# First MLP product of a Conformer layer by seven block products, with the residual stream kept in DRAM meanwhile

## The chip, the core and the metric

The kernel runs on one core of a Trainium2 chip. A core has five engines that work side by side, each on its own list of instructions in the order in which the list was written: PE (matrix products; its weight loads are shown apart as PEld), DVE (vector work), ACT (activations and copies), POOL (slower vector work) and SP (which here only issues transfers). They meet through semaphores. The metric is the device time of one execution in microseconds (us), the median of three runs; one further execution was profiled.

## The reference

One layer on 512 tokens of width 2048, all in float32, then a last RMSNorm:

```python
h = rmsnorm(x, norm1_g)
x = x + conformer_conv(h, ...)                  # w_in, GLU, 31-tap conv, layernorm, silu, w_out
x = x + square(relu(rmsnorm(x, norm2_g) @ w1)) @ w2   # w1 2048 x 8192, w2 8192 x 2048
return rmsnorm(x, final_g)
```

The change concerns the product with `w1` and what stands right before and behind it.

## The kernel before, in words

**Number format.** Every matrix product is split for accuracy: each operand becomes a high part (a cast to float32r) and a low part (the operand less its high part), and `mm3` (L282) adds three matmuls in one PSUM bank: high x high, high x low, low x high. Each of the three loads its own 128x128 stationary block.

**Stages.** The w_in projection and the convolution come first, then the w_out projection, whose first column group is done in a hand-written order with `ps`, and whose other three groups (q = 1 to 3, from L750) leave the residual stream `xt` with features on partitions (16 tiles of 128 features x 512 tokens). Then the first MLP product: `h2` holds the 16 tiles, scaled by the norm's gain and split into high and low (L768); for each of 64 blocks of 128 hidden features (`f`, L796) 16 x 3 matmuls of 128x512 sum over the 16 k-tiles into one bank. After the first block come the row scales of the norm (`row2`) and 64 transposes that turn `xt` into the residual with tokens on partitions, 16 tiles `x2` that stay in SBUF as `acc`.

**Hidden activations.** DVE applies relu and the row scale (L829), ACT squares (L830). Two blocks make a pair (32 pairs, 256 hidden features each). For 30 of the pairs, POOL forms four sums of the pair's blocks of 256 tokens (`s1` to `s4`, L840 to L843), ACT casts the seven factors to their high parts, DVE makes the low parts, and both are written to DRAM (`spill`). The second product needs them in that form.

**Second MLP product.** It already works by seven block products (`seven`, L856): a product of 2x2 blocks is formed with seven block products in place of eight, at the cost of sums on both sides. The factors of w2 are made while it runs: `Factor.make` (L153) forms differences on POOL (`less`, L158, 128x1024 in place), casts on ACT (L177), and for the low part either subtracts on POOL (`LO_POOL`, L179) or lets ACT copy the high part to PSUM twice (L183, bank `ax`) and DVE subtract in halves (L184). The activations' factors come back from `spill` by `fetch` (L789), issued on POOL into seven slots; three slots (pairs 0 to 2) are filled during the first product (at f = 8, 10, 12), pairs 3 to 6 from its end on.

**What sets the order.** `Stream` (L186) makes weight tiles four items ahead of their use; there are four buffers each for the high and the low parts (`wh`, `wl`), so the buffer of an item is the one that was used four items before. `LOAD` issues loads three items further ahead on SP. Outside the hand-written part (`manual_schedule`) a list scheduler orders each engine's instructions by the program order and by its own estimates; the engines then keep to that order.

Of the kernel before, what the change touches and what calls it, by code (L numbers as in the profile page):

```python
# [18 lines left out]
P = 128  # L19
# [49 lines left out]
LO_POOL = ("P2",)  # L69
# [13 lines left out]
def trunk(ctx: ExitStack, tc: tile.TileContext, xT, vec, fg, w_in, w_out, w1, w2s, w2b, out):  # L83
# [7 lines left out]
    big = ctx.enter_context(tc.tile_pool(name="big", bufs=16))  # L91
# [7 lines left out]
    early = right.enter_context(tc.tile_pool(name="early", bufs=1, side="right"))  # L99
    dram = ctx.enter_context(tc.tile_pool(name="dram", bufs=1, space=bass.MemoryType.DRAM))  # L100
# [26 lines left out]
    class Sums:  # L127


        def __init__(self, src):  # L130
            self.src = src
            self.raw = {}

        def buffer(self, b):

            pool, tag, n = (wts, "raw", 4) if b in ("22", "5") else (mlp[0], "rb", 8)
            return pool.tile([P, 1024], F32, tag=tag, name=f"b{b}", bufs=n)

        def get(self, b, hs):
            if (b, hs) not in self.raw:  # L140
                self.raw[b, hs] = t = self.buffer(b)
                nc.sync.dma_start(out=t, in_=self.src[BLOCKS.index(b), hs])
            return self.raw[b, hs]

    class Factor:
        def __init__(self, sums, product, hs):
            self.sums, self.product, self.hs = sums, product, hs
# [5 lines left out]
        def make(self, hi, lo):  # L153
# [24 lines left out]
            if self.product in LO_POOL:  # L178
                nc.gpsimd.tensor_tensor(out=lo, in0=s, in1=hi.bitcast(F32), op=sub)  # L179
                return  # L180
# [32 lines left out]
    for f in range(FF // P):  # L213
        items += [Plain(w1[f, c], nc.gpsimd if c else nc.vector) for c in range(2)]
    for g in range(NG):
        for q in range(2):
            sums = Sums(w2s[g, q])
# [3 lines left out]
    mlp = [None]  # L221
# [16 lines left out]
    mean1 = early.tile([P, P], F32, name="mean1")  # L238
# [4 lines left out]
    us = [early.tile([P, KC - 1 + T], F32, name=f"u{i}") for i in range(NU)]  # L243
# [46 lines left out]
    acc2 = early.tile([P, T], F32, name="acc2")  # L290
# [36 lines left out]

    def conv(j, pool_taps):

        u = us[j % NU]  # L330
        dj = big.tile([P, T], F32, tag="da", name=f"d{j}")
# [5 lines left out]
        for k in range(pool_taps):  # L337
            a, w = tap(k)
            prod = early.tile([P, T], F32, tag="prod", name="prod", bufs=3)
# [6 lines left out]
            if pacc is None:  # L346
                pacc = early.tile([P, T], F32, tag="pacc", name="pacc", bufs=2)
# [42 lines left out]
    with tc.manual_schedule():  # L390
# [45 lines left out]
        row1 = early.tile([P, T], F32, tag="row", name="row1", bufs=2)  # L436
# [24 lines left out]
    diags = early.tile([P, max(*PE_TAPS, 1), P], F32, tag="dg", name="dg", bufs=1)  # L461
# [19 lines left out]
    dl = big.tile([P, T], F32, tag="da", name="dl")  # L481
    held = None

    class Half:
# [30 lines left out]
        def act_taps(self, lo, hi):  # L515
            for k in range(lo, hi):
                a, w = self.tap(k)
                prod = early.tile([P, H], F32, tag="prod", name="prod", bufs=3)
                nc.scalar.activation(out=prod, in_=a, func=AF.Copy, scale=w)
                if k == 0:  # L520
                    self.pacc = early.tile([P, H], F32, tag="pah", name="pah", bufs=2)
# [74 lines left out]
        def put(self, i, cols):  # L596
# [6 lines left out]
            if i == 0:  # L603
                self.mean = early.tile([P, H], F32, tag="row", name="mean", bufs=2)
                nc.scalar.copy(out=self.mean, in_=self.rows[:, :H])
# [143 lines left out]
    h2 = [None] * NT  # L749
    for q in range(4):  # L750
        if q:
            ps = [bank() for _ in range(4)]
            for c in range(8):
                w = chunk()
                for i in range(2):
                    k = 2 * c + i
                    out_mm(ps, [x[:, i * 512 : (i + 1) * 512] for x in w], k, slice(0, T), k == 0, k == NT - 1)
        for n in range(4):
            j = 4 * q + n
            nc.vector.scalar_tensor_tensor(out=xt[j], in0=ps[n], scalar=col(V_BOUT, j), in1=xt[j], op0=ALU.add, op1=ALU.add)  # L760
            if j == 0:
# [5 lines left out]
    for j in range(NT):  # L767
        h2[j] = split_scaled(xt[j], col(V_G2, j), "y")  # L768


    NPAIR = FF // P // 2
    LASTS = NPAIR - GROUP // 4
    spill = [dram.tile([P, 2, 7 * HT], F32, name=f"spill{n}") for n in range(NPAIR)]
    acc = []
    row2 = None
    pairs = {}
    later = []

    def split(n, x, sl):

        width = sl.stop - sl.start
        hi = mlp[0].tile([P, 4 * HT], F32R, tag="rb", name="ah", bufs=8)
        lo = mlp[0].tile([P, 4 * HT], F32R, tag="rb", name="al", bufs=8)
        nc.scalar.copy(out=hi[:, :width], in_=x)
        nc.scalar.dma_start(out=spill[n][:, 0, sl], in_=hi[:, :width].bitcast(F32))
        nc.vector.tensor_tensor(out=lo[:, :width], in0=x, in1=hi[:, :width].bitcast(F32), op=ALU.subtract)
        later.append((spill[n][:, 1, sl], lo[:, :width].bitcast(F32)))

    def fetch(n):  # L789
# [3 lines left out]
        for y in range(2):  # L793
            nc.gpsimd.dma_start(out=pairs[n][y], in_=spill[n][:, y, :])

    for f in range(FF // P):  # L796
        ps = bank()
        for c in range(2):
            wh, wl = chunk()
            for i in range(8):  # L800
                k = 8 * c + i
                sl = slice(i * P, (i + 1) * P)
                mm3(ps, (wh[:, sl], wl[:, sl]), h2[k], k == 0, k == NT - 1)
        if row2 is None:
# [4 lines left out]
            r2 = spread(inv_sqrt(ms, eps_rms, RMS_EPS, NTOK))  # L809
            row2 = shift  # L810
            nc.scalar.copy(out=row2, in_=r2)

            for b in range(NTOK):
                for n in range(4):
                    x2 = big.tile([P, 512], F32, tag="da", name=f"x2_{b}_{n}")
                    pt = bank("ax")
                    for i in range(4):
                        nc.tensor.transpose(out=pt[:, i * P : (i + 1) * P], in_=xt[4 * n + i][:, b * P : (b + 1) * P], identity=ident)  # L818
                    nc.scalar.copy(out=x2, in_=pt)
                    acc.append(x2)  # L820
            right.close()
            mlp[0] = ctx.enter_context(tc.tile_pool(name="mlp", bufs=4, side="right", reuse_waits="tile"))
            slots = [ctx.enter_context(tc.tile_pool(name="slots", bufs=1, side="right", reuse_waits="tile"))] * 2
            slots.append(right.enter_context(tc.tile_pool(name="slot", bufs=1, side="right", reuse_waits="tile")))
        n = f // 2
        if f % 2 == 0:
            four = mlp[0].tile([P, 4 * HT], F32, tag="rb", name="four", bufs=8)
        here = four[:, f % 2 * T :][:, :T]
        nc.vector.scalar_tensor_tensor(out=here, in0=ps, scalar=0.0, in1=row2, op0=ALU.max, op1=ALU.mult)  # L829
        nc.scalar.activation(out=here, in_=here, func=AF.Square)  # L830
        for x in later:
            nc.scalar.dma_start(out=x[0], in_=x[1])
        later = []
        if n >= LASTS:
            split(n, here, slice(f % 2 * T, f % 2 * T + T))
        elif f % 2:
            a21, a11, a22, a12 = (four[:, i * HT : (i + 1) * HT] for i in range(4))
            sums = mlp[0].tile([P, 4 * HT], F32, tag="rb", name="sums", bufs=8)
            s3, s1, s2, s4 = (sums[:, i * HT : (i + 1) * HT] for i in range(4))
            nc.gpsimd.tensor_tensor(out=s3, in0=a11, in1=a21, op=ALU.subtract)  # L840
            nc.gpsimd.tensor_tensor(out=s1, in0=a21, in1=a22, op=ALU.add)
            nc.gpsimd.tensor_tensor(out=s2, in0=s1, in1=a11, op=ALU.subtract)
            nc.gpsimd.tensor_tensor(out=s4, in0=a12, in1=s2, op=ALU.subtract)  # L843
            split(n, four[:, HT:], slice(0, 3 * HT))
            split(n, sums, slice(3 * HT, 7 * HT))
        if f in (8, 10, 12):
            fetch((f - 8) // 2)
    for x in later:
        nc.scalar.dma_start(out=x[0], in_=x[1])
    left.close()  # L850
    late = ExitStack()
    slots += [late.enter_context(tc.tile_pool(name="slots2", bufs=1, reuse_waits="tile"))] * (SLOTS - 3)
    fetch(3)


# [35 lines left out]
    for g in range(NG - 1):  # L891
        for q in range(2):
# [3 lines left out]
    right.close()  # L896
    lasts = [ctx.enter_context(tc.tile_pool(name="lasts", bufs=1, side="right", reuse_waits="tile")),
             ctx.enter_context(tc.tile_pool(name="lasts2", bufs=1, reuse_waits="tile"))]
# [3 lines left out]
    def last_pair(n):  # L902
        for f in range(2):
            both = [lasts[0].tile([P, T], F32R, name="ah", tag=f"ah{len(a)}"),
                    lasts[0].tile([P, T], F32R, name="al", tag=f"al{len(a)}") if len(a) < 3 else mlp[0].tile([P, T], F32R, tag="rb", name="al", bufs=8)]
# [4 lines left out]
    for q in range(2):  # L910
        seven(NG - 1, q, 1)
        last_pair(LASTS + q)
        for n in (2 * q, 2 * q + 1):
            for m in range(4):
                raw = wts.tile([P, 1024], F32, tag="raw", name="raw", bufs=4)
                nc.sync.dma_start(out=raw[:, :512], in_=w2b[n, m])
                wh = lasts[1].tile([P, 512], F32R, tag=f"wh{n}{m}", name="w2h")
                wl = lasts[1].tile([P, 512], F32R, tag=f"wl{n}{m}", name="w2l")
# [10 lines left out]
    for b in range(NTOK):  # L929
# [6 lines left out]
        for i, cs in enumerate(pieces):  # L936
# [9 lines left out]
            sq = mlp[0].tile([P, 1024], F32, tag="rb", name="sq", bufs=8)  # L946
# [61 lines left out]
```

## Time and profile before

| What | Value |
|---|---|
| median of 3 runs (lowest, highest) | 1926.92 us (1924.57, 1929.64) |
| profiled execution: own time | 1929.75 us |
| profiled execution: span, first to last instruction | 1928.0 us |
| first MLP product, first to last matmul | 583.4 to 1290.2 us |
| second MLP product begins | 1290.9 us |
| DMA, mean over the span | 163 GB/s |

How to read it: the span lies between the first and the last instruction, and the rest of the execution's own time lies around it. Busy times of the engines overlap each other. A matmul's duration covers its way through the array, and the next one starts before it ends, so that the distance between two starts, not the duration, says what a row of matmuls takes. A group's line gives the instruction's line in the kernel, engine, operation, what it writes and reads with shapes, the count, the summed busy time, the mean of one in ns, and the idle time of the engine right before them with what ended it.

### The profile page before, as it was taken

The page shows a single profiled execution, that of the slowest core. Times are in us where ns is not written, and L with a number is a line of the kernel's source. Part 1 is how long each engine was busy: PE and PEld are TensorE (multiplying, and loading weights), DVE is VectorE, ACT ScalarE, POOL GpSimd, SP SyncE. Part 2 cuts the span into 40 slices and gives each one's busy share as a digit, 9 for nine tenths or more (in the row PEclk, how much of TensorE's full clock was granted, in tenths as well). Part 3 has the DMA queues.
Part 4 walks back from the last instruction along what each step waited for, and adds up shares of the span by engine and source line. Part 5 has one row for each costly group of instructions (what it writes and reads, how often), then busy time and mean ns, then how long its engine had stood idle before and what let it go on. Part 6 is the DMA issues. An engine that isn't in the chain of part 4 may idle for free.

```text
span 1928.0 us, 23365 instructions
## 1 busy us (share of the span) xinstructions
PE 1885.7 (98%) x8578; PEld 1565.3 (81%) x8578; DVE 1073.4 (56%) x1512; ACT 934.8 (48%) x1286; POOL 1122.3 (58%) x693
## 2 busy tenths in 40 slices
PE   6999999989999999999999999999999999999998
PEld 4888888988888888888888888887888888788776
DVE  8899999982034333332333333336665666556685
ACT  6444444464245333333333333346776677667762
POOL 5799999846553433434343333457567666686643
PEclk9999999989999999999999999999999999999999
DMA  5222233105222754554445544466746557457332
GB/s 217 84 99 88 99 120 113 63 13 206 98 95 101 272 199 174 183 195 181 178 172 187 193 175 175 181 215 232 250 143 240 193 189 274 132 217 245 127 103 98
DMA packets 87955, 314.33 MB, mean 163 GB/s; under 512 B 9760, under 2 KB 10400, under 8 KB 87840
## 3 DMA queue, kind: packets, MB, share of 16 engines
q1 hardware_dynamic: 59184, 197.41, 29.4%
q0 software_dynamic: 9792, 57.15, 8.4%
q10 hardware_dynamic: 18864, 58.27, 7.5%
q8 instruction: 67, 1.10, 0.2%
q14 instruction: 48, 0.39, 0.1%
HBM read 251.45 MB, written 61.34 MB: 162 GB/s over the span
## 4 chain that ended last, share of the span: by engine, by line
PE 84%; DVE 8%; POOL 4%; issue 3%; ACT 1%; DMA 1%; DVEq 0%; SPq 0%; POOLq 0%; ACTq 0%
PE mm L286 25%; PE mm L287 25%; PE mm L285 25%; PE mm L656 8%; POOL b L158 2%; DVE ax L361 1%; POOL wl L179 1%; DVE wl L184 1%; DVE x L874 1%; DVE xl L279 1%; DVE dl L545 1%; PE ax L818 0%; DMA b<-in_w2s 0%; DVE d L623 0%; DVE wl L125 0%
## 5 line engine op out<-in xcount | busy, mean ns | idle before, releaser
L125 POOL TENSOR_TENSOR wl<-raw,wh 128x1024 fp32r<-128x1024 f32 x151 | 365.5, 2431 | 464.1 <-ACT wh L124 447.6
L124 ACT CAST wh<-raw 128x1024 fp32r<-128x1024 f32 (+1 forms) x221 | 230.3, 1049 | 471.3 <-PE mm L286 369.2
L286 PE MATMUL mm<-yl,wh 128*128 128x512 f32 x1024 | 398.7, 389 | 0.2 <-DVE yl L279 0.2
L285 PE MATMUL mm<-yh,wh 128*128 128x512 f32 x1024 | 398.7, 389 | 0.0
L287 PE MATMUL mm<-yh,wl 128*128 128x512 f32 x1024 | 398.6, 389 | 0.0
L158 POOL TENSOR_TENSOR b<-b,b 128x1024 f32<-128x1024 f32 x120 | 288.7, 2417 | 148.7 <-DVE wl L184 83.5
L286 PE MATMUL mm<-wl,ah 128*128 128x512 f32 x840 | 327.7, 390 | 8.9 <-POOL wl L179 8.9
L285 PE MATMUL mm<-wh,ah 128*128 128x512 f32 x840 | 327.2, 390 | 1.2 <-DVE x L874 1.2
L287 PE MATMUL mm<-wh,al 128*128 128x512 f32 x840 | 326.7, 389 | 0.0
L184 DVE TENSOR_TENSOR wl<-b,ax 128x512 fp32r<-128x512 f32 x360 | 232.3, 684 | 129.4 <-ACT ax L183 115.1
L177 ACT CAST wh<-b 128x1024 fp32r<-128x1024 f32 x210 | 219.8, 1053 | 166.5 <-PE mm L287 149.2
L286 PEld LDWEIGHTS mm<-yl,wh 128*128 128x128 f32 x1024 | 192.2, 188 | 40.3 <-DVE yl L279 0.6
L285 PEld LDWEIGHTS mm<-yh,wh 128*128 128x128 f32 x1024 | 192.2, 188 | 39.8
L287 PEld LDWEIGHTS mm<-yh,wl 128*128 128x128 f32 x1024 | 192.2, 188 | 39.7
L361 DVE SCALAR_TENSOR_TENSOR ax<-u,v,ax 128x512 f32<-128x512 f32 x327 | 218.2, 753 | 0.0
L285 PE MATMUL mm<-xh,wh 128*128 128x512 f32 (+1 forms) x544 | 207.6, 382 | 5.1 <-ACT wh L124 5.1
L287 PE MATMUL mm<-xh,wl 128*128 128x512 f32 (+1 forms) x544 | 207.3, 381 | 4.0 <-DVE wl L125 4.0
L286 PE MATMUL mm<-xl,wh 128*128 128x512 f32 (+1 forms) x544 | 207.9, 382 | 1.6 <-DVE xl L279 1.6
L183 ACT COPY ax<-wh 128x512 f32<-128x512 f32 x360 | 200.3, 585 | 10.8 <-DVE wl L184 7.7
L874 DVE TENSOR_TENSOR x<-x,mm 128x512 f32<-128x512 f32 x224 | 149.6, 684 | 83.9 <-PE mm L287 83.9
L286 PEld LDWEIGHTS mm<-wl,ah 128*128 128x128 f32 x840 | 157.7, 188 | 44.5 <-POOL wl L179 12.2
L125 DVE TENSOR_TENSOR wl<-raw,wh 128x1024 fp32r<-128x1024 f32 (+1 forms) x70 | 87.9, 1256 | 184.1 <-ACT wh L124 184.1
(173 smaller groups left out, 2402.4 us busy)
## 6 DMA issues: line engine op xcount, KB each, us to landing
raw<-in_w SPq DMA_DIRECT2D x128, 512.0 KB, 3.2
b<-in_w2s SPq DMA_DIRECT2D x120, 512.0 KB, 4.5
raw<-in_w_in SPq DMA_DIRECT2D x63, 512.0 KB, 3.2
ah<-spill POOLq DMA_DIRECT2D x30, 896.0 KB, 5.7
al<-spill POOLq DMA_DIRECT2D x30, 896.0 KB, 8.0
raw<-in_w_out SPq DMA_DIRECT2D x32, 512.0 KB, 3.3
spill<-ah ACTq DMA_DIRECT2D x30, 512.0 KB, 2.6
spill<-al ACTq DMA_DIRECT2D x30, 512.0 KB, 2.7
```

The lines of the kernel that those rows point to most:

```text
L124: nc.scalar.copy(out=hi[:, sl], in_=raw[:, sl])
L125: (nc.vector if sl.stop == cut else self.eng).tensor_tensor(out=lo[:, sl], in0=raw[:, sl], in1=hi[:, sl].bitcast(F32), op=ALU.subtract)
L158: nc.gpsimd.tensor_tensor(out=raw[to, hs], in0=raw[x, hs], in1=raw[y, hs], op=sub)
L177: nc.scalar.copy(out=hi, in_=s)
L183: nc.scalar.copy(out=st, in_=hi[:, sl].bitcast(F32))
L184: nc.vector.tensor_tensor(out=lo[:, sl], in0=s[:, sl], in1=st, op=sub)
L285: nc.tensor.matmul(out=ps, lhsT=wh, rhs=xh, start=first, stop=False, **how)
L286: nc.tensor.matmul(out=ps, lhsT=wh, rhs=xl, start=False, stop=False, **how)
L287: nc.tensor.matmul(out=ps, lhsT=wl, rhs=xh, start=False, stop=last, **how)
L361: nc.vector.scalar_tensor_tensor(out=o, in0=a, scalar=w, in1=c, op0=ALU.mult, op1=ALU.add)
L656: nc.tensor.matmul(out=ps[n][:, sl], lhsT=a[:, wsl], rhs=x[:, sl], start=first and a is wh and x is hi, stop=last and x is lo)
L874: nc.vector.tensor_tensor(out=x2, in0=x2, in1=banks[x][s], op=ALU.add)
```

## The change

The first MLP product is done by seven block products too. The 16 k-tiles are taken as 8 pairs; `factors(p)` (new) scales a pair's two tiles on ACT, forms four sums of 128x256 on POOL, and then, for each of seven factors of 256 tokens, a high part on ACT and a low part on DVE. The weights come as `w1s`, four blocks of 128x1024 for each of 32 pairs of hidden blocks, and are made into seven factors by the same `Factor` code as w2 (products P2 and P3 take their low parts on POOL). A product of a pair is 8 x 3 matmuls of 128x256; seven of them, in three banks X, Y and Z, make a pair's four result blocks. DVE reads a bank after each product (L857 to L869 of the changed kernel), some reads twice over because a further sum is wanted.

The residual is transposed during the w_out projection (`residual`, 16 transposes for each column group) and is written to DRAM from ACT's queue; it is read back by 16 transfers on SP's queue after the first MLP product. All fetches of pairs 0 to 6 stand behind the first product. Buffers are laid out anew for this (`fore`, `prep`, `stage`, `res`).

```diff
+FIRST = (("P1", "P5", "P2", "P6", "P3", "P7", "P4"), ("P1", "P5", "P6", "P2", "P7", "P3", "P4"))
-LO_POOL = ("P2",)
+LO_POOL = (("P2", "P3"), ("P2",))
...
-    for f in range(FF // P):
-        items += [Plain(w1[f, c], nc.gpsimd if c else nc.vector) for c in range(2)]
+    for n in range(NPAIR):
+        sums = Sums(w1s[n], LO_POOL[0])
+        items += [Factor(sums, x) for x in FIRST[n > 0]]
...
+    def factors(p):
+        x = prep.tile([P, 4 * HT], F32, tag="x", name="xs", bufs=2)
+        for i in range(2):
+            nc.scalar.activation(out=x[:, i * T : (i + 1) * T], in_=xt[2 * p + i], func=AF.Copy, scale=col(V_G2, 2 * p + i))
...
+        nc.gpsimd.tensor_tensor(out=s1, in0=a21, in1=a22, op=ALU.add)
...
+            nc.scalar.copy(out=t[:, :HT], in_=f)
+            nc.vector.tensor_tensor(out=t[:, HT:], in0=f, in1=t[:, :HT].bitcast(F32), op=ALU.subtract)
+    def residual(n):
+        for b in range(NTOK):
...
+            nc.scalar.copy(out=x2, in_=pt)
+            nc.scalar.dma_start(out=acc[b][n], in_=x2)
...
+                    if q == 3 and k % 2 and k < 12:
+                        factors(k // 2)
+                if c == 1:
+                    residual(q - 1)
...
-    for j in range(NT):
-        h2[j] = split_scaled(xt[j], col(V_G2, j), "y")
...
-    for f in range(FF // P):
-        ps = bank()
...
-                mm3(ps, (wh[:, sl], wl[:, sl]), h2[k], k == 0, k == NT - 1)
+    for n in range(NPAIR):
+        banks = {x: bank() for x in "XYZ"}
...
+                mm3(x, tuple(h[:, sl] for h in w), (t[:, :HT], t[:, HT:]), product in OPENS and p == 0, p == 7, skip_group_check=True)
...
+                part(product, range(8), w)
+                read(product)
...
+        for x in (odd, even):
+            nc.scalar.activation(out=x, in_=x, func=AF.Square)
...
+            nc.gpsimd.tensor_tensor(out=s1, in0=z["21"], in1=z["22"], op=ALU.add)
...
-        if f in (8, 10, 12):
-            fetch((f - 8) // 2)
...
-    fetch(3)
+    for p in range(4):
+        fetch(p)
+    x2 = {}
+    for n in range(4):
+        for b in range(NTOK):
+            x2[b, n] = res.tile([P, 512], F32, name=f"acc{b}{n}")
+            nc.sync.dma_start(out=x2[b, n], in_=acc[b][n])
```

How the instructions stand now is shown for POOL and ACT in the middle of the first MLP product. Line numbers are those of each kernel's own file. First POOL before, one pair of hidden blocks: `wl` are low parts of w1, `sums` the four sums of the pair `four`.

```order
L125 TENSOR_TENSOR wl_6537<-raw_6538,wh_6536 128x1024
L840 TENSOR_TENSOR sums_6634<-four_6566 128x256
L125 TENSOR_TENSOR wl_6603<-raw_6604,wh_6602 128x1024
L841 TENSOR_TENSOR sums_6634<-four_6566 128x256
L842 TENSOR_TENSOR sums_6634<-sums_6634,four_6566 128x256
L843 TENSOR_TENSOR sums_6634<-four_6566,sums_6634 128x256
```

POOL now, one pair: `b11`, `b21`, `b12`, `b5`, `b22` are blocks of w1 and differences of them, `z` the finished pair of hidden blocks.

```order
L162 TENSOR_TENSOR b11_6480<-b22_6548,b5_6624 128x1024
L183 TENSOR_TENSOR wl_6696<-b21_6585,wh_6695 128x1024
L162 TENSOR_TENSOR b21_6585<-b21_6585,b11_6480 128x1024
L907 TENSOR_TENSOR sums_6730<-z_6478,z_6479 128x256
L908 TENSOR_TENSOR sums_6730<-z_6478 128x256
L909 TENSOR_TENSOR sums_6730<-sums_6730,z_6478 128x256
L910 TENSOR_TENSOR sums_6730<-z_6479,sums_6730 128x256
L183 TENSOR_TENSOR wl_6786<-b22_6548,wh_6785 128x1024
L162 TENSOR_TENSOR b5_6890<-b12_6783,b11_6746 128x1024
L162 TENSOR_TENSOR b12_6783<-b22_6814,b12_6783 128x1024
```

Where a pair had two 128x1024 operations and four small ones, it now has six and four (the two at the end belong to the pair after; that pair's own `b11` comes next), and the low part from `wh_6785` stands behind the sums.

ACT before, one pair: casts of w1 (`wh`), squares of `four`, casts and transfers of the pair's factors (`ah`, `spill`).

```order
L124 CAST wh_6572<-raw_6574 128x1024
L124 CAST wh_6602<-raw_6604 128x1024
L830 ACTIVATE four_6566<-four_6566 128x512
L784 CAST ah_6639<-four_6566 128x768
L785 DMA spill9_5030<-ah_6639 128x768
L784 CAST ah_6644<-sums_6634 128x1024
L832 DMA spill9_5030<-al_6640 128x768
L785 DMA spill9_5030<-ah_6644 128x1024
L124 CAST wh_6650<-raw_6652 128x1024
```

ACT now, at the same place: `ax` are the copies of high parts into PSUM.

```order
L181 CAST wh_6659<-b11_6480 128x1024
L181 CAST wh_6695<-b21_6585 128x1024
L187 COPY ax_6663<-wh_6659 128x512
L187 COPY ax_6666<-wh_6659 128x512
L900 ACTIVATE z_6479<-z_6479 128x512
L900 ACTIVATE z_6478<-z_6478 128x512
L914 CAST ah_6728<-z_6479 128x512
L914 CAST ah_6728<-z_6478 128x256
```

And right behind that:

```order
L181 CAST wh_6748<-b12_6517 128x1024
L914 CAST ah_6728<-sums_6730 128x1024
L187 COPY ax_6752<-wh_6748 128x512
L187 COPY ax_6755<-wh_6748 128x512
L181 CAST wh_6785<-b22_6548 128x1024
L181 CAST wh_6816<-b21_6585 128x1024
```

The cast of the sums (`ah_6728<-sums_6730`) now has copies of one weight factor and the cast of the next behind it in ACT's list, and the cast `wh_6695` stands right behind the cast of `b11_6480`, a block that POOL has just formed.

More of the change, by code (lines that the diff above doesn't have):

```diff
@@ L242, in trunk @@
     NU = 3
-    us = [early.tile([P, KC - 1 + T], F32, name=f"u{i}") for i in range(NU)]
+    us = [fore.tile([P, KC - 1 + T], F32, name=f"u{i}") for i in range(NU)]
     for u in us:
@@ L603, in put @@
             if i == 0:
[L604 removed]
+                self.mean = fore.tile([P, H], F32, tag="row", name="mean", bufs=2)
                 nc.scalar.copy(out=self.mean, in_=self.rows[:, :H])
@@ L808, in trunk @@
             nc.vector.tensor_scalar(out=ms, in0=st[:, :NTOK], scalar1=1.0 / D, scalar2=None, op0=ALU.mult)
[L809 to L830, printed above, removed]
+            nc.scalar.copy(out=row2, in_=spread(inv_sqrt(ms, eps_rms, RMS_EPS, NTOK)))
+        late = []
+        for product in FIRST[n > 0]:
+            w = chunk()
+            if n == 0 and product in LATE:
+                part(product, range(6), w)
+                late.append((product, w))
+                if product != LATE[-1]:
+                    continue
+                part("P1", (6, 7), late[0][1])
+                read("P1")
+                rows()
+                for x in late[1:]:
+                    part(x[0], (6, 7), x[1])
+                    read(x[0])
+            else:
+                part(product, range(8), w)
+                read(product)
         for x in later:
@@ L833, in trunk @@
         later = []
+        for x in (odd, even):
+            nc.scalar.activation(out=x, in_=x, func=AF.Square)
+        hi, lo = (stage.tile([P, 7 * HT], F32R, tag=x, name=x) for x in ("ah", "al"))
         if n >= LASTS:
[L835 to L838, printed above, removed]
+            parts = [(even, 0), (odd, 2)]
+        else:
+            sums = big.tile([P, 4 * HT], F32, tag="rb", name="sums")
```

162 lines of the change are left out of this document (104 added, 58 removed).

## The prediction

> **What bounds the kernel now.** I read the page's first part, then the busy time by stage, then the groups of instructions, each shape apart, and last the timeline. The page's first line names the engine:
>
> ```profile
> PE 1885.7 (98%) x8578; PEld 1565.3 (81%) x8578; DVE 1073.4 (56%) x1512; ACT 934.8 (48%) x1286; POOL 1122.3 (58%) x693
> ```
>
> By stage (start:end, length, then busy us of PE, PEld, DVE, ACT, POOL, granted clock, DMA share, GB/s), first the two product stages, w1 and then w2:
>
> ```profile
> 583.40:1290.90 707.50, 707.34 (x3153) 584.70 (x3152) 229.21 (x206) 244.24 (x285) 285.35 (x200) 1.00 0.50 184
> 1350.00:1875.00 525.00, 518.82 (x2280) 426.74 (x2279) 342.39 (x536) 374.38 (x526) 343.67 (x189) 1.00 0.55 193
> ```
>
> In the stage that is changed PE never waits, and POOL and ACT are busy for 40% and 35% of it. In the w2 stage, which already works by seven products, they are busy for 65% and 71%, and PE waits a little. What a matmul costs is read from the distance of two starts (start, duration), for 512 and for 256 columns; the 256-column ones are those of the convolution's last tile:
>
> ```profile
> 347.02 0.39 PE L285 MATMUL mm<-xh,wh 128*128 128x512 f32 x1
> 347.24 0.39 PE L286 MATMUL mm<-xl,wh 128*128 128x512 f32 x1
> 347.47 0.39 PE L287 MATMUL mm<-xh,wl 128*128 128x512 f32 x1
> ...
> 366.13 0.28 PE L286 MATMUL mm<-xl,wh 128*128 128x256 f32 x1
> 366.25 0.28 PE L287 MATMUL mm<-xh,wl 128*128 128x256 f32 x1
> 366.37 0.28 PE L285 MATMUL mm<-xh,wh 128*128 128x256 f32 x1
> ```
>
> So 0.227 and 0.120 us. The stage's 3 x 1024 matmuls take 3072 x 0.227 = 697 us of its 707.5; the other 10 are the 64 transposes and the row scales.
>
> **Part 1, PE's work.** Now 32 pairs x 7 products x 8 x 3 = 5376 matmuls at 0.120 = 645 us, 20.16 per pair. One product in eight is saved (87 us), but two half-length matmuls take 0.240, 0.013 more than a long one, so 52 us remain. The Trainium skill's page "TensorE: Matmul & The Clock Gate", section "Back-to-back issue gap", gives N/2.4 + 2.5 ns for a warm isolated gap, 109 ns for 256 columns and 216 for 512; by it the 5376 would take 586 us. The rows above have 120 and 227, with a weight load for each matmul, so the trace decides against that figure.
>
> **Part 2, who must keep up.** A pair now needs seven weight factors in 20.16 us, made by three engines. The prices are in the second product and in the sums of before (busy us, mean ns, idle before):
>
> ```profile
> L158 POOL TENSOR_TENSOR b<-b,b 128x1024 f32<-128x1024 f32 x120 | 288.7, 2417 | 148.7 <-DVE wl L184 83.5 <-DMA b<-in_w2s 55.1 <-issue 5.8
> L179 POOL TENSOR_TENSOR wl<-b,wh 128x1024 fp32r<-128x1024 f32 x30 | 71.9, 2398 | 43.0 <-ACT wh L177 43.0
> L841 POOL TENSOR_TENSOR sums<-four 128x256 f32<-128x256 f32 x30 | 43.5, 1452 | 0.0
> L843 POOL TENSOR_TENSOR sums<-four,sums 128x256 f32<-128x256 f32 x30 | 22.1, 737 | 2.4
> L177 ACT CAST wh<-b 128x1024 fp32r<-128x1024 f32 x210 | 219.8, 1053 | 166.5 <-PE mm L287 149.2 <-PE mm L286 13.2 <-DVE x L874 3.2
> L183 ACT COPY ax<-wh 128x512 f32<-128x512 f32 x360 | 200.3, 585 | 10.8 <-DVE wl L184 7.7
> L784 ACT CAST ah<-sums 128x1024 fp32r<-128x1024 f32 x30 | 31.5, 1051 | 124.7 <-POOL sums L843 124.7
> ```
>
> POOL, per pair: 4 differences x 2.417 + 2 low parts (P2, P3) x 2.398 + 4 sums x 0.737 = 17.4 us; with one sum at 1.452, as when DVE worked beside it, 18.1. That is under 20.16, but POOL has to wait twice in each pair, and both waits follow from the order. First: the low part of P3 stands behind the sums in POOL's list, and its high part stands in ACT's list behind the cast of those sums and the two copies of P7. From the last sum to that low part POOL stands still for 1.051 + 2 x 0.585 + 1.053 = 3.3 us. Second: the low part of P2 follows the difference for P6 in POOL's list, and ACT casts P6's factor, which POOL has just formed, before P2's: 2 x 1.053 = 2.1 us. ACT waits for POOL's sums and POOL for ACT, and neither passes over what waits. ACT's idle 124.7 us ahead of the cast of the sums shows it held there already, 4.2 us for each of 30, then without harm. The hand-overs are in the timeline:
>
> ```profile
> 904.22 0.74 POOL L842 TENSOR_TENSOR sums<-sums,four 128x256 f32<-128x256 f32 x1
> 905.04 0.74 POOL L843 TENSOR_TENSOR sums<-four,sums 128x256 f32<-128x256 f32 x1
> 905.81 1.05 ACT L784 CAST ah<-sums 128x1024 fp32r<-128x1024 f32 x1 [4.16 <-POOL sums L843]
> 905.87 0.33 ACTq L832 DMA_DIRECT2D spill<-al  x1
> ```
>
> 0.08 us from POOL to its own dependent next, 0.03 from POOL to ACT; some 14 steps at about 0.05 are 0.7. The ring of POOL and ACT closes in 17.4 to 18.1 + 3.3 + 2.1 + 0.7 = 23.5 to 24.2 us. P6's difference also overwrites the block whose low part DVE makes for P1, a wait that before does not show in this stage: 0 to 0.6. I take 24.0, with 22.8 (no hand-overs) and 24.8 as ends. PE then stands still for 3.8 us per pair, at P7 above all, which waits for its low part: DVE makes that behind the low part of the sums. The stage takes 32 x 24.0 = 768.
>
> DVE and ACT beside that:
>
> ```profile
> L184 DVE TENSOR_TENSOR wl<-b,ax 128x512 fp32r<-128x512 f32 x360 | 232.3, 684 | 129.4 <-ACT ax L183 115.1 <-issue 10.4 <-POOL wl L179 2.7
> L786 DVE TENSOR_TENSOR al<-sums,ah 128x1024 fp32r<-128x1024 f32 x30 | 36.8, 1226 | 100.3 <-ACT ah L784 100.3
> L628 DVE TENSOR_TENSOR d<-d,ax 128x256 f32<-128x256 f32 x30 | 12.4, 414 | 0.7 <-PE ax L602 0.7
> L830 ACT ACTIVATE four<-four 128x512 f32<-128x512 f32 x64 | 40.1, 626 | 0.0
> ```
>
> DVE: 10 half low parts x 0.684, 10 short reads of banks x 0.414, low parts of 1792 columns at 1.226 for 1024: 13 us. ACT: 7 casts x 1.053, 10 copies x 0.585, 2 squares x 0.626, casts of 1792 columns at 1.051 for 1024, 2 issues x 0.33: 17 us. Both fit and cost nothing beyond the ring. SP's loads of w1 keep their number and size.
>
> **Part 3, the start of the stage.** Each `factors(p)` has 2 scalings, 7 casts and 7 low parts of 128x256; the nearest rows:
>
> ```profile
> L278 ACT ACTIVATE yh<-xr,v 128x512 fp32r<-128x512 f32 x16 | 11.3, 722 | 14.3 <-PE mm L656 14.3
> L631 ACT CAST vh<-vj 128x256 fp32r<-128x256 f32 x32 | 13.0, 407 | 1.0
> L818 PE MATMUL ax<-ident,xr 128*128 128x128 f32 x64 | 9.3, 285 | 0.0
> ```
>
> ACT: 2 x 0.722 + 7 x 0.407 = 4.3 us. The last two, behind the final column group, are 8.6, covered by the first three products over six of eight k-pairs, 3 x 18 x 0.120 = 6.5; with the sums behind them I take 6 us of waiting (0 to 12). Stage: 774, against 707.5, +66.
>
> **Part 4, the w_out stage** takes over 48 of the 64 transposes: 48/64 x 9.3 = 7 us on PE, which the 774 above no longer holds. ACT has 6 x 4.3 = 26 us of factors in the last group's 192 x 0.227 = 43.6, beside casts, 16 issues x 0.33 for the residual's transfers and the copies that empty the transposes' two banks: a little waiting. +8 (5 to 14).
>
> **Part 5, the start of the second product.** Before, pairs 0 to 2 lay ready and 3 to 6 were fetched at its start:
>
> ```profile
> 1290.90:1322.00 31.10, 31.10 (x139) 25.75 (x138) 20.75 (x32) 23.90 (x34) 14.37 (x13) 1.00 0.96 349
> ```
>
> Waits in the second product (total, times, longest), and one of the page's DMA rows:
>
> ```profile
> POOL b L158 <- DMA b<-in_w2s: 52.4, 8, 12.0
> ...
> PE mm L286 <- POOL wl L179: 8.9, 7, 2.5
> ```
>
> ```profile
> ah<-spill POOLq DMA_DIRECT2D x30, 896.0 KB, 5.7
> ```
>
> The transfers were full there (0.96, 349 GB/s), POOL waited up to 12.0 us for weights, and PE lost 2.5 at most in one wait. Three more pairs (3 x 2 x 896 KB) and 16 residual tiles of 256 KB are 9.7 MB, 28 us at that rate, and the 16 reads stand on SP ahead of the next weights. Four weight factors made ahead cover 4 x 12 x 0.227 = 11; I take +15, ends 0 and 28. The last group and the end load and compute as before under the same products: 0.
>
> **Sum.** 1928.0 + 66 + 8 + 15 = 2017 us of span. The profiled execution has 1.75 us around its span and lies 2.8 above the median: 2017 + 1.75 - 2.8 = 2016.
>
> **The rivals.**
>
> *PE keeps the bound* (the other side). If POOL's two waits overlap with stock made ahead, a pair costs PE's 20.16, since POOL's 17.4 to 18.1 fits: stage 645 + 6, that is -56; with +8 and +7: 1928 - 41, less 1.1 for the median, 1886. It decides where the ring stays under 20.16, thus at under 2 us of waits. For it: the w2 stage runs near PE's pace with 65% of POOL. Against: there POOL has 5 long operations per seven factors, not 6 and four sums, and nothing that ACT must hand back in between. By the page's 109 ns it would be 59 us less, 1827. Chance 0.08.
>
> *Only the first wait counts*, the second falling into time that POOL would lose anyway: 17.75 + 3.3 + 0.3 = 21.4 per pair, stage 691, -16; with 8 and 15: 1934. For it: buffers are four deep. Chance 0.10, half of it inside 0.3%.
>
> *The clock falls.* PE's waits of 3.8 us come once in 24. Stretches of 3.4 us, with the clock's figure third from the end:
>
> ```profile
> 414.20:417.60 3.40, 1.22 (x8) 1.02 (x9) 3.29 (x7) 1.01 (x2) 1.12 (x1) 0.99 0.00 0
> 417.60:421.00 3.40, 3.40 (x19) 3.40 (x18) 2.62 (x8) 3.02 (x7) 0.73 (x1) 0.50 0.02 5
> 421.00:424.40 3.40, 3.40 (x17) 3.40 (x18) 1.67 (x8) 2.55 (x5) 1.49 (x2) 0.50 0.00 0
> ...
> 1335.70:1339.10 3.40, 1.76 (x8) 1.44 (x9) 0.02 (x1) 0.15 (x1) 3.32 (x2) 1.00 0.00 0
> ```
>
> With PE busy for 1.22 of 3.40 the clock was halved for the next 6.8; with 1.76 it was not. A wait of 3.8 would halve it for at least one stretch in most pairs: 1.7 us more of PE. In the ring that falls mostly into PE's spare time; where it does not (P4's end frees the buffer of P2), 32 x 1.7 = 54 more: 2070. The same page of the Trainium skill, section "Part 1: The HAM clock gate", has the clock fall after an idle window of about 3.4 us; by that, waits which straddle two windows would leave it alone. Here a third of a window's work did not prevent it. Chance 0.12.
>
> That the change does not do what it says has no chance worth a number: the matmuls are counted in the order.
>
> **How the numbers follow.** Forecast 0.70, 2016. Its ends: ring 730 to 794, start 0 to 12, transposes 5 to 14, transfers 0 to 28, all low 1954, all high 2067; not all fall together. With the clock's case, the range is 1960 to 2075; the first two rivals stay outside. About 0.3% is what a measurement of this kernel can tell. Faster 0.08; same 0.05, from the second rival; slower 0.87.
>
> **What would show it.** Right: PE busy about 84% in the w1 stage, with one gap of 3 to 4 us per pair at P7, one pair every 24 us; POOL idle twice per pair, for ACT's casts; the stage some 770 long; DMA near 350 GB/s and waits for `spill` or residual tiles at the second product's start. Wrong: pairs every 20.2 us with PE without gaps, or a stage of 24 us whose gaps follow DMA or DVE alone.

## The result, and the profile after

The changed kernel takes 2047.13 us (median of 4, 2045.88 to 2050.01), the kernel before 1926.13 us in the same comparison (median of 4): a ratio of 1.063, interval 1.061 to 1.065, 121 us slower. The forecast was 2016, with 1960 to 2075 as its range. The sign, and the mechanism of the main term, came out as forecast; the size was 31 us short.

The page's first part has PE busy for about as long as before, in a longer span:

```profile
PE 1894.5 (93%) x10882; PEld 1681.9 (82%) x10882; DVE 1331.2 (65%) x2094; ACT 1204.6 (59%) x1788; POOL 1449.0 (71%) x853
```

The busy time by stage (start:end, length, PE, PEld, DVE, ACT, POOL, granted clock, DMA share, GB/s): the first pair of w1, its next 30 pairs, the last pair, and from there to the end:

```profile
597.57:640.01 42.44, 31.03 (x202) 29.13 (x201) 24.67 (x48) 28.95 (x52) 22.39 (x18) 0.80 0.22 75
640.01:1364.52 724.51, 648.60 (x5043) 640.94 (x5042) 418.59 (x690) 453.39 (x660) 535.29 (x301) 0.94 0.46 163
1364.52:1388.50 23.98, 21.84 (x170) 21.67 (x169) 15.28 (x25) 15.40 (x23) 17.32 (x10) 0.93 0.65 228
1388.50:2044.80 656.30, 625.87 (x2727) 513.50 (x2725) 411.48 (x650) 427.05 (x621) 414.63 (x234) 0.98 0.57 198
```

A pair takes 724.51 / 30 = 24.15 us; the forecast was 24.0. POOL is busy for 535.29 / 30 = 17.8 of them, as the prices of before had it (17.4 to 18.1), and PE's 168 matmuls need 20.16 at the full clock. So neither is full. The waits between 666 and 1342 us, which hold 28 pairs (who waits for whom, total, times, longest):

```profile
POOL wl L183 <- ACT wh L181: 147.5, 56, 3.1
ACT ah L914 <- POOL sums L910: 130.7, 28, 4.7
...
PE mm L293 <- DVE wl L188: 39.2, 18, 3.0
...
PE mm L291 <- ACT wh L181: 28.7, 10, 4.3
```

POOL waits for ACT's casts exactly twice in a pair (56 in 28), and ACT once for POOL's sums. PE stands still once in a pair, at P7, as forecast, but for 67.9 / 28 = 2.4 us on average and not 3.8, and it is busy for 648.60 / 724.51 = 90% instead of 84%: at a granted clock of 0.94 its matmuls take up a part of its spare time. One pair in POOL's timeline (start, duration; the idle time before it and what ended it in brackets):

```profile
1054.21 2.41 POOL L162 TENSOR_TENSOR b<-b,b 128x1024 f32<-128x1024 f32 x1 [0.48 <-DVE wl L188]
1058.73 2.42 POOL L183 TENSOR_TENSOR wl<-b,wh 128x1024 fp32r<-128x1024 f32 x1 [2.11 <-ACT wh L181]
...
1063.59 1.19 POOL L907 TENSOR_TENSOR sums<-z 128x256 f32<-128x256 f32 x1
...
1066.43 0.74 POOL L910 TENSOR_TENSOR sums<-z,sums 128x256 f32<-128x256 f32 x1
1070.31 2.41 POOL L183 TENSOR_TENSOR wl<-b,wh 128x1024 fp32r<-128x1024 f32 x1 [3.14 <-ACT wh L181]
1072.69 4.90 POOL L162 TENSOR_TENSOR b<-b,b 128x1024 f32<-128x1024 f32 x2
1078.06 2.41 POOL L162 TENSOR_TENSOR b<-b,b 128x1024 f32<-128x1024 f32 x1 [0.47 <-DVE wl L188]
```

The difference for P6 (1054.21), 2.11 of waiting, P2's low part, P4's difference, the four sums, 3.14 of waiting, P3's low part, the next pair's differences for P5 and P7, and its P6 again 23.85 later. The forecast had 2.1, 3.3 and, for DVE, 0 to 0.6. ACT's side of the longer wait shows what stands between the last sum and P3's cast:

```profile
1067.20 1.04 ACT L914 CAST ah<-sums 128x1024 fp32r<-128x1024 f32 x1 [4.70 <-POOL sums L910]
1068.16 1.10 ACT L187 COPY ax<-wh 128x512 f32<-128x512 f32 x2
1069.19 2.94 ACT L181 CAST wh<-b 128x1024 fp32r<-128x1024 f32 x3
```

Two places cost more than forecast. At the start, PE waits once in the last column groups of the w_out stage and several times in the first pair. In front of the waits of 6.53 and 3.26 stands a cast of ACT that waits for POOL's sums of the activation factors; the 2.95 the trace puts down to DVE's low parts of weights. ACT first, then PE:

```profile
557.59 0.41 ACT L784 CAST y<-ysums 128x256 fp32r<-128x256 f32 x1 [4.49 <-POOL ysums L779]
...
619.74 0.41 ACT L784 CAST y<-ysums 128x256 fp32r<-128x256 f32 x1 [1.90 <-POOL ysums L777]
```

```profile
563.35 1.97 PE L793 MATMUL ax<-ident,xr 128*128 128x128 f32 x8 [6.53 <-ACT x L795]
...
606.08 1.08 PE L793 MATMUL ax<-ident,xr 128*128 128x128 f32 x4 [2.95 <-DVE wl L188]
...
620.20 0.58 PE L291 MATMUL mm<-y,wh 128*128 128x256 f32 x1 [3.26 <-ACT y L784]
```

At the second product's start the transfers are full (1.03 in the row's last column but one), SP is held for 34 us by the residual's 16 reads, and a weight issued right behind them reaches POOL 25 us later. The stretch, then SP, POOL, and PE's waits there, which add up to 18.1 us (to 3.9 in the kernel before):

```profile
1391.00:1422.00 31.00, 22.48 (x74) 16.60 (x75) 15.81 (x12) 8.54 (x13) 23.04 (x18) 0.78 1.03 382
```

```profile
1383.45 34.05 SPq L934 DMA_DIRECT2D acc<-x  x16
1417.61 56.03 SPq L146 DMA_DIRECT2D b<-in_w2s  x12
```

```profile
1442.60 11.85 POOL L162 TENSOR_TENSOR b<-b,b 128x1024 f32<-128x1024 f32 x5 [26.53 <-DMA b<-in_w2s]
```

```profile
PE mm L292 <- POOL wl L183: 7.4, 1, 7.4
...
PE mm L291 <- DMA ah<-spill: 6.0, 2, 3.6
...
PE mm L293 <- DMA al<-spill: 4.7, 2, 3.1
```

### The profile page after: what moved, and what is told of

The parts are those of the page before. It is cut to its first block, busy times and chain, and to the rows that moved or that the text cites. A ratio compares the mean times of both kernels' runs of the same rounds, so it can differ in the third digit from the quotient of the medians.

```text
span 2044.8 us, 29355 instructions
## 1 busy us (share of the span) xinstructions
PE 1894.5 (93%) x10882; PEld 1681.9 (82%) x10882; DVE 1331.2 (65%) x2094; ACT 1204.6 (59%) x1788; POOL 1449.0 (71%) x853
## 4 chain that ended last, share of the span: by engine, by line
PE 58%; POOL 17%; DVE 12%; ACT 6%; issue 4%; DMA 2%; POOLq 0%; SPq 0%; ACTq 0%; DVEq 0%
PE mm L293 17%; PE mm L291 17%; PE mm L292 17%; POOL b L162 6%; PE mm L669 5%; POOL wl L183 4%; DVE ax L374 4%; ACT wh L181 3%; POOL sums L907 2%; POOL sums L908 1%; DVE wl L188 1%; ACT ah L914 1%; POOL sums L910 1%; POOL sums L909 1%; DVE al L915 1%
## 5 line engine op out<-in xcount | busy, mean ns | idle before, releaser
L162 POOL TENSOR_TENSOR b<-b,b 128x1024 f32<-128x1024 f32 x248 | 596.5, 2413 | 198.2 <-DMA b<-in_w2s 108.4
L181 ACT CAST wh<-b 128x1024 fp32r<-128x1024 f32 x434 | 445.3, 1048 | 297.9 <-PE mm L293 158.0
L188 DVE TENSOR_TENSOR wl<-b,ax 128x512 fp32r<-128x512 f32 x680 | 437.0, 682 | 230.3 <-ACT ax L187 213.2
L293 PE MATMUL mm<-y,wl 128*128 128x256 f32 x1792 | 527.7, 295 | 43.8 <-DVE wl L188 43.8
L291 PE MATMUL mm<-y,wh 128*128 128x256 f32 x1792 | 527.8, 295 | 41.9 <-ACT wh L181 28.7
L292 PE MATMUL mm<-y,wh 128*128 128x256 f32 x1792 | 525.1, 293 | 0.0
L293 PEld LDWEIGHTS mm<-y,wl 128*128 128x128 f32 x1792 | 362.9, 203 | 48.1 <-DVE wl L188 48.1
L291 PEld LDWEIGHTS mm<-y,wh 128*128 128x128 f32 x1792 | 363.0, 203 | 46.4 <-ACT wh L181 34.2
L187 ACT COPY ax<-wh 128x512 f32<-128x512 f32 x680 | 379.5, 585 | 27.5 <-DVE wl L188 21.2
L183 POOL TENSOR_TENSOR wl<-b,wh 128x1024 fp32r<-128x1024 f32 x94 | 226.4, 2408 | 204.1 <-ACT wh L181 204.1
L292 PEld LDWEIGHTS mm<-y,wh 128*128 128x128 f32 x1792 | 362.6, 202 | 0.3 <-DVE y L785 0.2
L291 PEld LDWEIGHTS mm<-wh,ah 128*128 128x128 f32 x840 | 159.6, 190 | 45.4 <-ACT ax L187 6.5
```

What stands on the lines that cost most here:

```text
L162: nc.gpsimd.tensor_tensor(out=raw[to, hs], in0=raw[x, hs], in1=raw[y, hs], op=sub)
L181: nc.scalar.copy(out=hi, in_=s)
L187: nc.scalar.copy(out=st, in_=hi[:, sl].bitcast(F32))
L188: nc.vector.tensor_tensor(out=lo[:, sl], in0=s[:, sl], in1=st, op=sub)
L291: nc.tensor.matmul(out=ps, lhsT=wh, rhs=xh, start=first, stop=False, **how)
L292: nc.tensor.matmul(out=ps, lhsT=wh, rhs=xl, start=False, stop=False, **how)
```

## The experiments

The theory: in the w1 stage POOL and ACT each keep to a list that makes them wait for the other, and the two waits with the work between them close a ring of 24 us, in which no engine is full. Its rivals: POOL's amount of work sets the pace; PE with a lowered clock sets it.

**Order alone (sums_late).** The cast of the activation sums is written behind the next pair's first products. On POOL nothing moves; in ACT's list that cast now comes behind the casts for P7 and P3.

```diff
-        for x, at in parts:
-            (cast to hi, low part to lo)
+        for x, at in parts[:2]:
+            store(hi, lo, x, at)
+        held = [(store, hi, lo, *x) for x in parts[2:]]   # done behind P2 of the next pair
```

> Only the order of ScalarE's list changes in the w1 stage: the cast of the activation sums (and its low part) comes behind the casts of the next pair's P7 and P3 factors; GpSimd's list and all the work stay. Ring of in-order waits: the wait of 3.1 us per pair between the last sum and the low part of P3 goes, 24.1 - 3.1 = 21.0 us per pair or PE's 20.2 if more is freed; 31 pairs, so 97 to 120 us less than the changed kernel's 2047: 1927 to 1950, PE almost without waits from the third pair on. GpSimd's amount of work sets the pace (17.9 us of operations that contention stretches): nothing changes, 2040 to 2050. The lowered clock sets it: the pairs shorten only as far as the clock is granted, about 6% of 750 us, 2000 or more.

Measured: 1961.14 us (median of 4), 1.018 of the kernel before (1.0165 to 1.0195), thus 86 less than the changed kernel. Its 30 pairs behind the first, the waits of 28 of them, and POOL at the place of the longer wait:

```profile
639.21:1274.72 635.51, 616.11 (x5042) 607.77 (x5042) 446.67 (x690) 452.30 (x660) 562.38 (x300) 1.00 0.53 185
```

```profile
POOL wl L183 <- ACT wh L181: 59.0, 28, 2.1
```

```profile
1118.15 0.74 POOL L915 TENSOR_TENSOR sums<-z,sums 128x256 f32<-128x256 f32 x1
1118.85 2.40 POOL L183 TENSOR_TENSOR wl<-b,wh 128x1024 fp32r<-128x1024 f32 x1
```

A pair takes 635.51 / 30 = 21.18 us. The wait of 3.14 is gone, that of 2.1 is left, once in each pair; POOL does the same work, and the pair is 2.97 us shorter. The same work in another order is 89 us faster over the 30 pairs, so POOL's load did not set the 24 us, and with the clock's 2000 or more it does not agree either. The total stays 11 above the range that the ring had promised: the wait brought its own price, but PE's 20.2 was not reached. What sets 21.18 seems to be POOL now: 562.38 / 30 = 18.7 of operations and 2.1 of waiting (its 128x1024 differences took 2.66 us in the mean, 2.41 in the changed kernel; DVE's low part of the sums now runs beside them). The clock comes back to 1.00 with PE's waits gone.

**Less work for POOL (p3_low_on_dve).**

```diff
-LO_POOL = (("P2", "P3"), ("P2",))
+LO_POOL = (("P2",), ("P2",))
```

> The low part of P3 is made by DVE in two halves, with two copies more on ScalarE, so GpSimd has 2.4 us less to do in each pair; the order is else kept. GpSimd's amount of work sets the pace: 31 x 2.4 = 75 us less, 1972. Ring: GpSimd no longer stands behind P3's cast, but its difference for P6 overwrites a block whose low part DVE makes from ScalarE's copies, and ScalarE's list from the sums' cast to those copies has grown by 1.2 us, so the wait moves there: 2025 to 2045, with a wait of GpSimd for DVE of 4 us or more in each pair.

Measured: 2098.61 us in one run, 51 more than the changed kernel. The 30 pairs, the waits of 27 of them, and POOL behind the sums:

```profile
642.63:1414.64 772.01, 668.38 (x5042) 662.17 (x5042) 483.80 (x750) 491.49 (x720) 483.71 (x272) 0.90 0.43 153
```

```profile
POOL b L162 <- DVE wl L188: 197.5, 27, 10.3
...
ACT wh L181 <- PE mm L292: 34.1, 23, 1.8
```

```profile
1064.98 5.89 POOL L162 TENSOR_TENSOR b<-b,b 128x1024 f32<-128x1024 f32 x2
1075.71 2.40 POOL L162 TENSOR_TENSOR b<-b,b 128x1024 f32<-128x1024 f32 x1 [4.84 <-DVE wl L188]
```

POOL's work fell to 483.71 / 30 = 16.1 us, and the pair grew to 25.73. POOL runs ahead to P6's difference and waits there for DVE (197.5 / 27 = 7.3 us on average, 4.84 in the pair shown), as the ring had it; that it came out slower, not a little faster, neither theory expected. In ACT's list 1.2 us of copies came in between, in DVE's list two half low parts, and DVE's low part of the sums, now beside POOL's differences, takes 2.48 us in place of 1.23:

```profile
1066.13 2.48 DVE L915 TENSOR_TENSOR al<-sums,ah 128x1024 fp32r<-128x1024 f32 x1 [0.84 <-ACT ah L914]
```

ACT, in turn, waits for PE to free weight buffers (34.1 us here, 22.6 in the changed kernel). How the 1.6 us divide among these was not separated. It refutes the load theory all the same: POOL was busy for 52 us less (535.29 to 483.71), and the kernel took 51 us more.

**Less work for PE (two_terms).** Of the three matmuls of each product the second is left out (and the third takes the activation's low part).

```diff
-                mm3(x, tuple(h[:, sl] for h in w), (t[:, :HT], t[:, HT:]), ...)
+                nc.tensor.matmul(out=x, lhsT=wh, rhs=t[:, :HT], ...)
+                nc.tensor.matmul(out=x, lhsT=wl, rhs=t[:, HT:], ...)
```

> Leaves out one of the three matmuls of each product block of the w1 stage (high weight by low activation), so a third of PE's work there; all factors are still made. Ring: PE is not in it, so the pairs keep 24 us and the time stays 2047, or at most the 18 us that the first pair lost shrink a little: 2030 to 2050. PE's matmuls with the lowered clock set the pace: 32 pairs x 56 x 0.120 = 215 us of matmuls go, and the time falls below 1950.

Measured: 2036.23 us in one run. The 30 pairs:

```profile
636.59:1351.56 714.97, 497.72 (x3363) 479.49 (x3362) 384.47 (x691) 450.31 (x660) 528.66 (x301) 0.86 0.46 164
```

23.83 us a pair: a third of PE's matmuls went, the clock fell to 0.86, and the pair is 0.3 shorter. That 0.3 lies in the first half of the stage, where single pairs of the changed kernel took up to 26.6 us; in the second half they took 23.8 there too. So PE is not in the ring, and the lowered clock falls into its spare time, but for 10 us at most over the 30 pairs.

**Two sums off POOL (two_sums_on_dve),** on top of the late cast: `s1` and `s3` on DVE.

```diff
-            nc.gpsimd.tensor_tensor(out=s1, in0=z["21"], in1=z["22"], op=ALU.add)
-            nc.gpsimd.tensor_tensor(out=s3, in0=z["11"], in1=z["21"], op=ALU.subtract)
+            nc.vector.tensor_tensor(out=s1, in0=z["21"], in1=z["22"], op=ALU.add)
+            nc.vector.tensor_tensor(out=s3, in0=z["11"], in1=z["21"], op=ALU.subtract)
```

> The late cast of the sums as in the run of 1961, and two of the four activation sums of each pair on DVE instead of GpSimd. If GpSimd's list is what keeps a pair there at 21.1 us (18.7 of operations, 2.1 of the wait for P2's cast and some hand-overs): 2.1 us of sums go, PE's 20.2 decides, 29 pairs x 0.9 = 26 less: 1932 to 1940. If ScalarE or DVE sets 21.1: 1955 to 1970.

Measured: 1937.54 us in one run, 24 less than the run of 1961:

```profile
641.31:1252.64 611.33, 608.01 (x5042) 605.69 (x5041) 479.26 (x750) 453.58 (x660) 522.38 (x241) 1.00 0.56 193
```

20.38 us a pair, PE busy for 99.5%: PE bounds the stage again, near its 20.16. So once the longer wait is gone POOL's load does count, as the last 0.8 us.

**The start (ysums_on_dve, no_transposes).** First the sums of the activation factors on DVE, in the changed kernel:

```diff
-        nc.gpsimd.tensor_tensor(out=s1, in0=a21, in1=a22, op=ALU.add)   # and s2, s3, s4
+        nc.vector.tensor_tensor(out=s1, in0=a21, in1=a22, op=ALU.add)
```

> The changed kernel, with the 32 sums of the activation factors before the w1 stage (four per pair of k-tiles) on DVE instead of GpSimd. If the start is late because ScalarE's casts of these sums stand and wait for GpSimd, which has weight factors and the squares' sums between them (5.9 and 5.3 us in one piece): the w_out stage gets 2 us shorter and the first pair 42.4 to 36 or 38, in all 2038 to 2042. If DVE, which makes the low parts there, is what is late: the sums make it later, 2047 to 2055.

Measured: 2037.28 us in one run, with the first pair at 36.49 instead of 42.44:

```profile
595.26:631.75 36.49, 28.06 (x202) 26.16 (x201) 23.67 (x53) 26.91 (x49) 13.40 (x8) 0.91 0.26 87
```

So 6 us of the late start, and the 2.3 us by which the stage now begins sooner (595.26 against 597.57), came from ACT's casts that waited for POOL. Then the transposes left out, with the copies and the transfers kept:

```diff
-                nc.tensor.transpose(out=pt[:, i * P : (i + 1) * P], in_=xt[4 * n + i][:, b * P : (b + 1) * P], identity=ident)
-            nc.scalar.copy(out=x2, in_=pt)
+            nc.scalar.copy(out=x2, in_=xt[4 * n + b])
```

> Leaves out the 64 transposes of the residual stream (ScalarE copies the same number of columns straight from the stream, so that the copies and the transfers stay, and what is stored is not turned). If PE's wait of 6.7 us in the w_out stage comes of the transposes, whose two banks ScalarE empties behind casts that wait for GpSimd: that wait, 48 x 0.11 of transposes and some 3 us of halved clock go, and the w_out stage is 12 to 15 us shorter (171 to 174, from 186.2). If the factors hold PE up there also without them: only the transposes' own 5 to 7 us go. The first pair loses 16 transposes and the waits around them, 4 to 7 us from 42.4, if it isn't the factors that it waits for. In all 2027 to 2040.

Measured: 2045.7 us in one run. The w1 stage begins at 590.08, 7.5 us earlier, and its first pair takes 45.32:

```profile
590.08:635.40 45.32, 30.02 (x185) 27.91 (x185) 29.08 (x56) 31.19 (x58) 25.50 (x22) 0.77 0.21 70
```

The time missed both expectations, being 1.4 less than the changed kernel's. Of the 7.5 us, 2.9 came back in the first pair, although it has 16 transposes less, and 2.4 in the 30 pairs behind it (726.88 against 724.51). In the first pair PE now waits longer for the factors' casts:

```profile
616.91 0.58 PE L291 MATMUL mm<-y,wh 128*128 128x256 f32 x1 [5.46 <-ACT y L784]
```

So the factors' casts hold the first pair; the transposes and the wait of 6.5 us in front of them hardly count in the total.

**The second product's start (no_reads, fetch_late).** The residual's reads left out, in the changed kernel:

```diff
-            nc.sync.dma_start(out=x2[b, n], in_=acc[b][n])
+            nc.vector.memset(x2[b, n], 0.0)
```

> Leaves out the 16 reads of the residual tiles at the second product's start (the tiles are set to zero by DVE instead), so that the weights behind them on SP are issued at once and 4.2 MB less is moved. If the reads ahead of the weights are what GpSimd's wait of 26.5 us and PE's of 7.4 us come from: 7 to 12 us less than the changed kernel, 2035 to 2040. If the seven pairs' fetches fill the transfers anyhow: 0 to 3 us less, 2044 to 2047.

Measured: 2042.13 us (median of 4; 1.0605 of before, 1.0587 to 1.0623, where the changed kernel has 1.0628, 1.0609 to 1.0647): some 5 less, between the two expectations, and the intervals overlap. Then, with the late cast of the sums, the fetches of pairs 4 to 6 moved behind POOL's low parts of the second half:

```diff
-                if (q, step) == FETCH[p]:
+                if (q, step) == (((0, 13), (1, 1), (1, 3), (1, 12)) if g == 0 else FETCH)[p]:
+    # and each of these fetches is issued behind POOL's last low part before it
```

> The late cast of the sums as in the run of 1961, and the fetches of pairs 4 to 6 issued behind GpSimd's low parts of the second half's weights instead of at the second product's start. If the full transfers make the weights late there (GpSimd waited 26.5 us, PE 9.1 us in one piece): PE's last wait goes, 1950 to 1953. If the cost is that the first pairs can be fetched only when the w1 stage's memory is free: no change, 1958 to 1962.

Measured: 1949.45 us in one run, 12 less than the run of 1961. PE's waits in the first 80 us of the second product, without and with the move:

```profile
PE mm L292 <- POOL wl L183: 8.9, 1, 8.9
...
PE mm L291 <- DMA ah<-spill: 7.0, 2, 5.1
...
PE mm L293 <- DMA al<-spill: 3.2, 2, 2.7
```

```profile
PE mm L293 <- DMA ah<-spill: 6.8, 2, 4.9
...
PE mm L295 <- DMA al<-spill: 3.3, 2, 2.6
```

The 8.9 us that PE waited for a weight are gone; the 10 us for the first pairs' factors stay. So the cost has two parts: pairs that are not needed yet crowd out the weights, and the first pairs' factors come late. Why they do was not tried by itself. That the w1 stage gives its memory back late, as the expectation had it, is not shown: in the changed kernel POOL issued the first pair's two fetches at 1380.68 and 1381.40, some 10 us before PE stood, and had no idle time in front of them; that the transfers were full then may as well be the reason.

**All together (combined).** The late cast, the two sums and the factors' sums on DVE, the late fetches, and the second half's 8 residual tiles read behind two of its weights.

> All together: late cast of the sums, two activation sums on DVE, the sums of the activation factors on DVE, the fetches of pairs 4 to 6 late, and the second half's 8 residual tiles read behind two weights of that half. With each at its own price (1961 - 26 - 6 - 9 - 2): 1918, so within 1% of the kernel before, and below it. If the pieces wait for the same thing: 1930 to 1945. Below 1905 the w1 stage would have to lose its start too.

Measured: 1916.44 us (median of 6, 1912.13 to 1919.67), 0.9938 of the kernel before (0.9924 to 0.9951): the fastest of all, with the seven products kept.

```profile
631.88:1243.30 611.42, 608.05 (x5043) 605.71 (x5042) 478.93 (x750) 453.48 (x660) 522.48 (x241) 1.00 0.57 193
```

Of the 52 us that the seven products save on PE, some 12 reach the end (1928.02, the kernel before in that comparison, less 1916.44). Most of the others go to the w_out stage (the w1 stage begins at 595.44 and not 583.40), to the first pair (36.44 us where the matmuls need 20.16) and to the second product, which takes some 10 us longer than before.

## Why the prediction was right, and where it was short

By its own terms, in the profiled spans (1928.0 and 2044.8, 116.8 apart; the sum had 89):

| Term | forecast | measured |
|---|---|---|
| w_out stage | +8 | 597.57 - 583.40 = +14.2 |
| ring, 32 pairs | 768 | 32 x 24.15 = 773 |
| start of the w1 stage | 6 | 42.44 + 724.51 + 23.98 - 773 = 18 |
| start of the second product | +15 | 656.3 - 637.1 = +19.2 |

**The ring** was right in its mechanism, its two waits and its size: 24.15 against 24.0. Breaking one wait by order alone took out what that wait was worth, and neither less POOL work nor less PE work did. In the sign that PE would be busy for 84%, the stretching of its matmuls by the clock was left out.

**The start** is the step that was mis-sized: 18 instead of 6, beyond its end of 12. The forecast counted ACT's own 8.6 us for the last two `factors` and took the products behind them as cover. But ACT's casts stood and waited for POOL, whose four sums came between weight factors and the sums of squares, each long; moving these sums to DVE took 6 of the 18 off. The row of before that should have been priced is POOL's, with its waits, not ACT's. The clock adds to it: it was granted at 0.80 in this pair, at 0.91 in the one of 36.49. PE stood for 42.44 - 31.03 = 11.4 us of the pair; how much of the rest is the clock and how much the waits was not separated.

**The w_out stage**: 14.2 instead of 8, at the upper end. All of it arises in the three column groups that carry the transposes: at their first matmul the changed kernel is 0.4 us ahead.

```profile
452.68 0.63 PE L656 MATMUL mm<-vh,wh 128*128 128x512 f32 x2
```

```profile
452.25 0.63 PE L669 MATMUL mm<-vh,wh 128*128 128x512 f32 x2
```

The first two groups take 2.1 us longer each, with 16 transposes each, so the 48 cost some 6.4 us, near the 7 that were said. The last group takes 10.4 longer: PE waited 6.5 us there for the transposes' banks, which ACT had to empty behind the casts that waited for POOL, and the clock was lowered around that wait (0.70 granted from 556.0 to 567.2).

**The second product's start**: +19 for +15, within its ends, and by the cause named (full transfers, weights behind other transfers); the residual's reads, 4.2 of the 9.7 MB that the forecast counted, turned out a small part of it, about 5.

**The rivals.** PE did not keep the bound: it comes near it only with the order changed and two sums off POOL (20.38 us a pair). That only the first wait counts is refuted by the 56 waits in 28 pairs. The clock did fall, as said (0.94 in the ring on average), and there it cost 0.3 us a pair at most: with a third of PE's work gone it fell to 0.86, and the pair took 23.83. The forecast's 54 us for it did not appear.

## What to carry to other kernels

Count not only each engine's work per step but follow its list: two engines that hand work to each other twice in a step can set the pace with neither full, and then the cure is the order of one of the lists, not less work. Where a new stage needs many small factors, price the engine that forms the first of them, with what stands ahead of it in its list. Fetch what is needed next first; transfers for later work that start early are paid for by the work in front.

## What the runs showed of the hardware

In the 30 pairs of the changed kernel the clock was halved 18 times, around waits of PE of 2.2 to 4.3 us. In one of these places PE was busy for 2.79 of 4.75 us, and the clock was halved for the 3.45 that followed:

```profile
699.00:703.75 4.75, 2.79 (x24) 2.59 (x22) 2.26 (x3) 3.35 (x5) 1.53 (x3) 1.00 0.46 190
703.75:707.20 3.45, 2.81 (x13) 2.84 (x14) 2.54 (x6) 2.72 (x4) 3.45 (x2) 0.51 0.98 317
```

```profile
704.39 0.55 PE L291 MATMUL mm<-y,wh 128*128 128x256 f32 x1 [2.60 <-ACT wh L181]
```

The Trainium skill's page "TensorE: Matmul & The Clock Gate", section "HAM oscillation — how this bites in real kernels", puts the limit at idle gaps of about 3.4 us. This trace does not agree: PE stood idle for 1.96 us in the first stretch and 0.64 in the second, 2.6 in one piece. Nor does the length of the wait alone decide: around another of 2.59 us, which ended at 728.64, PE was busy for only 0.41 of 3.00 us and the clock stayed at 1.00. What decides between the two is not shown here.

```profile
726.00:729.00 3.00, 0.41 (x4) 0.39 (x4) 2.97 (x6) 2.97 (x5) 1.23 (x1) 1.00 0.82 306
```

DVE and POOL slow each other when both have all their operands in SBUF: in the changed kernel the first sum of a pair took 1.19 us on POOL beside DVE's low parts where the last took 0.74, and in `p3_low_on_dve`, where DVE's low parts ran beside the last, it was 0.75 and 1.07. DVE's low part of 1024 columns took 2.48 us there beside POOL's differences, where its mean in the kernel before was 1.23. DVE's half low parts, which read one operand from PSUM, took 0.68 in the mean with POOL at work and without.
